# The modulation matrix's chunks leave the GLA stage for the two MLPs, and the first mixer takes its rest at a larger share

## The chip, the cores and the metric

The kernel runs on one core of a Trainium2 chip. The metric is the device time of one execution in microseconds (us); lower is better. Times of several executions are given as a median with the lowest and the highest.

## The reference, cut to what matters

Two transformer blocks of depth two run one after the other on 256 tokens of width 1024. The first block is attention, MLP, gated linear attention (GLA), MLP. The second block runs twice: a mixer (masked attention, a short convolution, gates) and a sparse expert stage. Before each of its two layers a conditioning vector `c` is turned into 6144 numbers, which shift, scale and gate that layer:

```python
# first block, depth 2
h = x
h = h + attention_mixer(rmsnorm(h, norm_mix[0]), ...)
h = h + sq_relu_mlp(rmsnorm(h, norm_mlp[0]), mlp_w_in[0], mlp_w_out[0])
h = h + gla_mixer(rmsnorm(h, norm_mix[1]), ...)
h = h + sq_relu_mlp(rmsnorm(h, norm_mlp[1]), mlp_w_in[1], mlp_w_out[1])
# second block, for l in range(2)
ada = (c @ w_ada[l] + b_ada[l])[:, None, :]
sh1, sc1, g1, sh2, sc2, g2 = jnp.split(ada, 6, axis=-1)
h = rmsnorm_2(x, norm1_g[l]) * (1.0 + sc1) + sh1
```

`w_ada` of both layers is 2 x 1024 x 6144 numbers of float32. It depends on nothing that the first block computes, so the kernel spreads `c @ w_ada` over the stages of the first block and the first mixer. The matrix is cut into 96 chunks of 128 rows x 1024 (512 KB each), 48 for each layer.

## The kernel before, in words

**Stages.** `run` goes through attention, MLP 0, GLA, MLP 1, mixer 0, expert stage 0, mixer 1, expert stage 1. Nearly all matmuls are products of a weight chunk with the activations. A weight chunk is 128 x 1024 float32 (512 KB), eight 128 x 128 tiles. `chunk` (L158 to L167) loads it on SP's queue into a buffer `raw`, lets ScalarE (ACT) round it to `whi` (L165) and VectorE (DVE) form the rest `wlo` (L166). `mm3` (L169 to L173) then takes three matmuls for each tile: `whi` with the high part of the activations (L171), `whi` with their low part (L172), `wlo` with the high part (L173). One chunk is 24 matmuls. There are 4 buffers `raw` and 3 each of `whi` and `wlo`; a load can only be issued when the chunk four loads before it has been used up.

**A modulation chunk** (`ada_steps`, L729 to L752) takes no matmul. Its load (L739) goes through the same 4 buffers `raw` and the same SP queue, and one DVE instruction multiplies it with `c` and sums along the row (L740) into one column of `mod`. L740 then frees the buffer.

**The background list.** The 96 modulation chunks are steps of the list `bg`, each at a cost of 1.14. Each time `lin` (L175) or `lin_nat` (L206) fetches a weight chunk it calls `bg.step(share)`, which adds `share` to a credit and issues steps from the list's head while the credit covers their cost. A share of 0.6 is about one modulation chunk for two weight chunks. `flush` issues whatever is left at once:

```python
def step(self, share):
    self.credit = self.credit + share if self.q else 0.0
    while self.q and self.credit >= self.q[0][0]:
        c, f = self.q.pop(0)
        self.credit -= c
        with self.net.tc.issue_after(self.net.last_lo):
            f()
```

`last_lo` is the `wlo` instruction of the weight chunk just fetched, so a modulation chunk is issued behind it. Within this the order of each engine's instructions is fixed when the program is built; at run time each engine goes through its own in order, and a waiting instruction holds those behind it.

**Who takes how many before.** MLP 0 (64 weight chunks, `MLP_SHARE` 0.6) takes 33 modulation chunks. The GLA stage replaces `bg` by a list of its own for its own DVE steps, and puts the first `GLA_ADA` = 8 modulation chunks behind them (L649); what that list has left when the last of the `wgin` chunks is fetched is flushed. The output projection of GLA (`wgo`, 8 weight chunks, L729) takes 4 more, MLP 1 takes 33, mixer 0 the last 18. Mixer 0 has 48 weight chunks ahead of its output projection `wout`; its list begins with 14 other steps of cost 0.45 (six empty ones, and eight that scale `x`, L775). With `MIX_SHARE` 0.45 its 47 calls give a credit of 21.2, of which 6.3 go to those steps and 14.9 to modulation chunks at 1.14 each: 13. The flush ahead of `wout` issues the other five. Mixer 1 runs the same code with an empty list.

**Names.** In the GLA stage, `v` and `r` come from `lin_nat` in PSUM and are taken out by L633, L634 (`vz`) and L643 to L645 (`sr`). The recurrence over the heads follows: L670 forms a state update, L677 (DVE) adds it to `st`; L684 forms scores, L685 (DVE) copies them under a mask to `at`. In mixer 0, L312 to L328 are the softmax, L829 the scores, L858 the copy of the transposed probabilities; L915 and L917 (DVE) form `ga`, L229 and L230 split it to `mh` and `ml`, which `wout` reads.

Of the kernel before, what the change touches and what calls it, by code (L numbers as in the profile page):

```python
# [20 lines left out]
T = 256  # L21
# [15 lines left out]
PACED = True  # L37
AHEAD = 100
WSLOTS = 4
MLP_SHARE = 0.6  # L40
MIX_SHARE = 0.45
U1_SHARE = 1.35
U2_SHARE = 1.45
V1_SHARE = 1.12
V2_SHARE = 0.52
DOTS = (8, 24)
SUMS = 4
GLA_ADA = 8
GSCALE = 2.0 ** 15
PACK = (("ones", 128), ("ident", 128), ("eps", 1), ("eps2", 1), ("one1", 1), ("gains64", 4), ("bada", 96))  # L50

# [49 lines left out]
class Net:  # L101
# [378 lines left out]
    def mlp(self, l):  # L480
        nc, a = self.nc, self.a
        with ExitStack() as st:
# [21 lines left out]
            self.early = factor  # L504
            self.lin(a["wmi"][l], 0, 32, 8, self.yh, self.yl, ev1, share=MLP_SHARE, n=T)
            if l == 0:
                self.next_norm(self.gain(1))
            else:
                while not self.ada0:
                    self.bg.q.pop(0)[1]()  # L510
                self.next_norm(self.gg, self.modc(0, 0), self.tot2, self.gain(4))
            self.lin(a["wmo"][l], 0, 8, 32, hh, hl, ev2, share=MLP_SHARE)


    def gla(self):
        nc, a, c, tc = self.nc, self.a, self.cst, self.tc
        with ExitStack() as st:
# [128 lines left out]
                                                   op0=ALU.add, op1=ALU.mult)  # L646
                return go

            self.bg.add(bg.q[:GLA_ADA])  # L649
            del bg.q[:GLA_ADA]  # L650
            for half in range(2):
                ci = self.lin_nat(a["wgin"], ci, 512, self.yh, self.yl, ev_v(half), 1.2)
            for half in range(2):
# [6 lines left out]
            oh, ol = [gp.tile([P, 8, T], F32R, tag=t, name=t) for t in ("oh", "ol")]  # L660
# [65 lines left out]
                pipe.push(h)  # L726
            pipe.drain()
            self.next_norm(self.gain(3))
            self.lin(a["wgo"], 0, 8, 8, oh, ol, self.add_x, n=T, share=MLP_SHARE)  # L729


    def ada_steps(self, l, i0, i1, cb):
# [48 lines left out]
    def mixer(self, l):  # L781
        nc, a, c, tc = self.nc, self.a, self.cst, self.tc
        with ExitStack() as st:
# [141 lines left out]
            ci = 0  # L925
            lin = lambda *args, **kw: self.lin(*args, share=MIX_SHARE, **kw)
            for nblk, ev in ((4, ev_k), (4, ev_v), (4, ev_q), (4, ev_c), (4, ev_h), (4, ev_b)):
# [558 lines left out]
```

## Time and profile before

| | before |
|---|---|
| device time, median of 3 (lowest to highest) | 2560.3 us (2559.42 to 2560.81) |
| the profiled execution's own time | 2562.75 us |
| its span in the profile | 2560.4 us |
| PE (matmul) busy | 2516.6 us, 98% |
| DVE busy | 2098.6 us, 82% |
| ACT busy | 1301.5 us, 51% |
| mean rate of all DMA | 221 GB/s |

The span runs from the first to the last instruction of the profiled execution; its own time has 2.35 us more around it. PE's busy time overlaps in itself, since matmuls are pipelined, so the places where it waits are read from its idle time, from the length of stages that do the same matmuls, and from the clock that it was granted, not from the busy share.

### The profile page before, as it was taken

How to read it: one execution, taken by the hardware profiler on the slowest of the kernel's cores; microseconds unless marked ns; L12 is line 12 of the kernel's file. 1: busy time of each engine (PE TensorE's matmuls, PEld its weight loads, DVE VectorE, ACT ScalarE, POOL GpSimd, SP SyncE). 2: the span in 40 equal slices, each digit the busy share in tenths (PEclk: the TensorE clock that was granted, in tenths of full speed). 3: DMA queues.
4: the chain of work that ended last, by engine and by line, in shares of the span. 5: the costliest groups of instructions: out<-in, count | busy, mean ns of one | idle time of the engine just before them, and what ended most of it. 6: DMA issues, size and time to landing. Idle time of an engine off the chain costs nothing.

```text
span 2560.4 us, 55126 instructions
## 1 busy us (share of the span) xinstructions
PE 2516.6 (98%) x22496; PEld 2461.7 (96%) x22496; DVE 2098.6 (82%) x3835; ACT 1301.5 (51%) x2031; POOL 182.3 (7%) x172
## 2 busy tenths in 40 slices
PE   8999999999998999999999999999999999999998
PEld 7799987999898999999999999999999999999998
DVE  7697687887787799889888777777798899888776
ACT  6654474554644645444444445645545444444444
POOL 0000100000000000321000121000000221000120
PEclk9999999999999999999999999999999999999999
DMA  5288754887477566877666887456566877666884
GB/s 191 86 293 281 253 183 153 268 275 264 149 251 234 159 195 200 295 259 247 212 185 203 265 296 242 140 178 197 165 191 204 299 249 265 194 190 199 280 296 164
DMA packets 155773, 566.47 MB, mean 221 GB/s; under 512 B 17680, under 2 KB 17904, under 8 KB 155264
## 3 DMA queue, kind: packets, MB, share of 16 engines
q1 hardware_dynamic: 135648, 490.97, 58.7%
q0 software_dynamic: 19872, 71.99, 9.0%
q8 instruction: 176, 2.88, 0.4%
q14 instruction: 77, 0.63, 0.1%
HBM read 561.83 MB, written 1.05 MB: 220 GB/s over the span
## 4 chain that ended last, share of the span: by engine, by line
PE 92%; DMA 3%; DVE 2%; ACT 1%; issue 1%; POOL 0%; SPq 0%; DVEq 0%; ACTq 0%
PE b L171 29%; PE b L173 29%; PE b L172 28%; PE b L1234 1%; PE b L1235 1%; DVE wlo L166 1%; DMA rows<-in_un,idx 1%; PE b L1181 1%; ACT whi L165 0%; DMA raw<-in_wmi 0%; PE b L829 0%; DMA raw<-in_wada 0%; DMA x<-in_xT 0%; PE b L426 0%; DMA A<-in_sel 0%
## 5 line engine op out<-in xcount | busy, mean ns | idle before, releaser
L171 PE MATMUL b<-yh,whi 128*128 128x224 f32 (+3 forms) x5336 | 1484.4, 279 | 12.1 <-ACT whi L165 11.4
L172 PE MATMUL b<-yl,whi 128*128 128x224 f32 (+3 forms) x5336 | 1476.2, 277 | 2.0 <-DVE yl L225 2.0
L173 PE MATMUL b<-yh,wlo 128*128 128x224 f32 (+3 forms) x5336 | 1476.2, 277 | 1.7 <-DVE wlo L166 1.5
L165 ACT CAST whi<-raw 128x1024 fp32r<-128x1024 f32 x829 | 868.4, 1049 | 1128.1 <-PE b L172 962.1
L166 DVE TENSOR_TENSOR wlo<-raw,whi 128x1024 fp32r<-128x1024 f32 x829 | 1009.9, 1220 | 260.0 <-ACT whi L165 254.6
L171 PEld LDWEIGHTS b<-yh,whi 128*128 128x128 f32 (+1 forms) x5336 | 1021.3, 192 | 17.5 <-ACT whi L165 12.7
L172 PEld LDWEIGHTS b<-yl,whi 128*128 128x128 f32 (+1 forms) x5336 | 1022.4, 192 | 4.9 <-DVE yl L225 2.4
L173 PEld LDWEIGHTS b<-yh,wlo 128*128 128x128 f32 (+1 forms) x5336 | 1021.0, 192 | 3.6 <-DVE wlo L166 2.7
L172 PE MATMUL b<-hl,whi 128*128 128x256 f32 x512 | 144.9, 283 | 0.0
L171 PE MATMUL b<-hh,whi 128*128 128x256 f32 x512 | 144.9, 283 | 0.0
L173 PE MATMUL b<-hh,wlo 128*128 128x256 f32 x512 | 144.9, 283 | 0.0
L1125 POOL DMA_INDIRECT rows<-in_un,idx x64 | 88.7, 1387 | 698.7 <-DVE gS L1093 411.1
L740 DVE CUSTOM_DVE_ANT_0 raw<-raw,c_cb 128x1024 f32<-128x1024 f32 x96 | 116.9, 1219 | 3.5 <-DMA raw<-in_wada 3.4
L1125 POOL DMA_INDIRECT rows<-in_ev,idx x64 | 69.4, 1084 | 613.7 <-DVE hN L1147 374.4
L172 PEld LDWEIGHTS b<-hl,whi 128*128 128x128 f32 x512 | 98.3, 192 | 0.0
L173 PEld LDWEIGHTS b<-hh,wlo 128*128 128x128 f32 x512 | 98.3, 192 | 0.0
L171 PEld LDWEIGHTS b<-hh,whi 128*128 128x128 f32 x512 | 98.3, 192 | 0.0
L1236 DVE TENSOR_TENSOR A<-A,b 128x512 f32<-128x512 f32 x112 | 73.5, 682 | 21.5 <-PE b L1235 21.3
L1206 ACT ACTIVATE A<-b 128x224 f32<-128x224 f32 x256 | 89.0, 348 | 0.0
L1136 DVE CUSTOM_DVE_ANT_0 rows<-rows,hN 128x1024 f32<-128x1024 f32 x64 | 78.0, 1219 | 12.4 <-DMA rows<-in_un,idx 12.4
L1147 DVE SCALAR_TENSOR_TENSOR hN<-rows,wS,hN 128x1024 f32<-128x1024 f32 x62 | 79.3, 1279 | 0.0
L1224 DVE TENSOR_TENSOR o<-oe,ghl 128x1024 f16<-128x1024 f16 x112 | 77.0, 688 | 1.7
(336 smaller groups left out, 2980.3 us busy)
## 6 DMA issues: line engine op xcount, KB each, us to landing
raw<-in_ut SPq DMA_DIRECT2D x256, 512.0 KB
raw<-in_ev SPq DMA_DIRECT2D x256, 512.0 KB
raw<-in_wada SPq DMA_DIRECT2D x96, 512.0 KB
raw<-in_win SPq DMA_DIRECT2D x80, 512.0 KB
raw<-in_wmi SPq DMA_DIRECT2D x64, 512.0 KB
raw<-in_wmo SPq DMA_DIRECT2D x64, 512.0 KB
raw<-in_wq SPq DMA_DIRECT2D x32, 512.0 KB
raw<-in_wgin SPq DMA_DIRECT2D x24, 512.0 KB
```

The costliest lines, as they stand in the source:

```text
L165: nc.scalar.copy(out=hi[:, :n], in_=raw[:, :n])
L166: self.last_lo = nc.vector.tensor_sub(out=lo[:, :n], in0=raw[:, :n], in1=hi[:, :n]).ins
L171: mm(out, lhsT=wh, rhs=yh, start=start, stop=False)
L172: mm(out, lhsT=wh, rhs=yl, start=False, stop=False)
L173: mm(out, lhsT=wl, rhs=yh, start=False, stop=stop)
L740: nc.vector.tensor_tensor_reduce(out=raw, in0=raw, in1=cb, op0=ALU.mult, op1=ALU.add, scale=1.0, scalar=0.0, accum_out=self.mod[:, i : i + 1])
L1125: nc.gpsimd.indirect_dma_start(out=got[g], out_offset=None, in_=a["un"] if name == "un" else a["ev"].rearrange("l i p d -> (l i p) d"), in ...
L1136: V.tensor_tensor_reduce(out=rows, in0=rows, in1=hN, op0=ALU.mult, op1=ALU.add, scale=1.0, scalar=0.0, accum_out=wS[:, g : g + 1])
L1147: V.scalar_tensor_tensor(out=hN, in0=rows, scalar=wS[:, g : g + 1], in1=hN, op0=ALU.mult, op1=ALU.add)
L1206: nc.scalar.activation(out=A[i2 // HALF][:, i2 % HALF, :], in_=ps[:, :NT], func=AF.Gelu_apprx_tanh)
L1224: V.tensor_tensor(out=o2, in0=e.unsqueeze(1).to_broadcast([P, 2, ng, HALF, GK]), in1=gates.to_broadcast([P, 2, ng, HALF, GK]), op=ALU.mult)
L1236: V.tensor_tensor(out=A[half][:, :, ts], in0=A[half][:, :, ts], in1=m.rearrange("p t i -> p i t"), op=ALU.mult)
```

## The change

The share of the MLPs goes from 0.6 to 0.72, that of the mixers from 0.45 to 0.55. The GLA stage puts no modulation chunk into its own list any more, and `wgo` takes none. By the credit and by the order of the loads, MLP 0 now takes 39 chunks, MLP 1 takes 40 and mixer 0 the last 17, against 33, 33 and 18 before, with 12 in the GLA stage. The changed credit of mixer 0 is 47 x 0.55 = 25.9; less the 6.3 it leaves 19.6, enough for 17 chunks at 1.14. What is computed does not change.

```diff
-MLP_SHARE = 0.6
-MIX_SHARE = 0.45
+MLP_SHARE = 0.72
+MIX_SHARE = 0.55
...
-GLA_ADA = 8
...
-            self.bg.add(bg.q[:GLA_ADA])
-            del bg.q[:GLA_ADA]
             for half in range(2):
                 ci = self.lin_nat(a["wgin"], ci, 512, self.yh, self.yl, ev_v(half), 1.2)
...
-            self.lin(a["wgo"], 0, 8, 8, oh, ol, self.add_x, n=T, share=MLP_SHARE)
+            self.lin(a["wgo"], 0, 8, 8, oh, ol, self.add_x, n=T)
```

The first place is DVE at the end of the GLA stage's `wgin` chunks. Before, it stands like this (L740 with `raw` is a modulation chunk, L166 the `wlo` of a weight chunk; the line `mod_69` behind each L740 with `raw` reads its sum out):

```order
L740 ISA raw_4396,mod_69<-raw_4396,c_cb_1315 128x1024
...
L740 ISA raw_4405,mod_69<-raw_4405,c_cb_1315 128x1024
L740 ISA mod_69 128x1
L677 SCALAR_TENSOR_TENSOR st_4432<-st_4425,eb_3878,b7_4427 128x256
L740 ISA raw_4408,mod_69<-raw_4408,c_cb_1315 128x1024
...
L677 SCALAR_TENSOR_TENSOR st_4436<-st_4429,eb_3877,b0_4434 128x256
L740 ISA raw_4411,mod_69<-raw_4411,c_cb_1315 128x1024
...
L645 SCALAR_TENSOR_TENSOR sr_3665<-rt_4386,rt2_4388 128x512
L685 COPY_PREDICATED at_3666<-c_gmask_3651,b1_4441 128x128
```

In the changed kernel the same place reads as follows; lines after the two removed constants and statements have moved up by one to three, so that L644 is L645 of before, L674 is L677, L682 is L685 and L165 is L166:

```order
L165 TENSOR_TENSOR wlo_4699<-raw_4696,whi_4698 128x1024
L165 TENSOR_TENSOR wlo_4734<-raw_4731,whi_4733 128x1024
L644 SCALAR_TENSOR_TENSOR sr_3683<-rt_4398,rt2_4400 128x512
L674 SCALAR_TENSOR_TENSOR st_4430<-st_4423,eb_3895,b0_4428 128x256
L682 COPY_PREDICATED at_3684<-c_gmask_3669,b1_4435 128x128
L644 SCALAR_TENSOR_TENSOR sr_3683<-rt_4403,rt2_4405 128x512
L682 COPY_PREDICATED at_3688<-c_gmask_3669,b5_4469 128x128
L165 TENSOR_TENSOR wlo_4770<-raw_4767,whi_4769 128x1024
```

The modulation chunks are gone from between the instructions that the recurrence needs, and the `wlo` of the first `wgo` chunks have moved up to their place.

The second place is DVE at the end of mixer 0, just ahead of `wout`, where the flush stands before (`wlo_9463` is the first `wout` chunk, L745 the sum with the bias when all 48 chunks of a layer are in):

```order
L740 ISA raw_9440,mod_69<-raw_9440,c_cb_1315 128x1024
L740 ISA mod_69 128x1
L298 COPY scc_9387<-b5_9355 128x2
L299 TENSOR_TENSOR sct_9386<-b5_9355,rstd_7404 128x256
L740 ISA raw_9443,mod_69<-raw_9443,c_cb_1315 128x1024
...
L915 SCALAR_TENSOR_TENSOR ga_7362<-ga_7362,b6_9391 128x256
L740 ISA raw_9446,mod_69<-raw_9446,c_cb_1315 128x1024
...
L915 SCALAR_TENSOR_TENSOR ga_7362<-ga_7362,b7_9417 128x256
L917 TENSOR_TENSOR ga_7362<-ga_7362,gc_7363 128x256
L166 TENSOR_TENSOR wlo_9463<-raw_9460,whi_9462 128x1024
```

In the changed kernel the last modulation chunk (`raw_9413`) stands here (L737 is L740 of before, L742 is L745):

```order
L165 TENSOR_TENSOR wlo_9410<-raw_9407,whi_9409 128x1024
L737 ISA raw_9413,mod_69<-raw_9413,c_cb_1315 128x1024
L737 ISA mod_69 128x1
L229 SCALAR_TENSOR_TENSOR ml_7364<-ga_7365,mh_7363 128x256 x2
L297 COPY scc_9366<-b4_9334 128x2
L298 TENSOR_TENSOR sct_9365<-b4_9334,rstd_7407 128x256
L742 TENSOR_TENSOR mod_69<-mod_69,c_pack_67 128x48
L290 TENSOR_SCALAR wyh_9456<-mod_69 128x8 x2
L165 TENSOR_TENSOR wlo_9463<-raw_9460,whi_9462 128x1024
```

No chunk is left for the flush: one modulation chunk, behind the last weight chunk of the projections ahead of `wout`, in place of a run of them.

The third place is SP's queue near the start of MLP 0. Before it loads one modulation chunk after two weight chunks:

```order
L162 DMA raw_1526<-in_wmi 128x1024
L162 DMA raw_1563<-in_wmi 128x1024
L739 DMA raw_1569<-in_wada 128x1024
L162 DMA raw_1603<-in_wmi 128x1024
L162 DMA raw_1640<-in_wmi 128x1024
L739 DMA raw_1646<-in_wada 128x1024
```

In the changed kernel (L161 and L736 are L162 and L739 of before) it is after one and two in turn for most of the way:

```order
L161 DMA raw_1526<-in_wmi 128x1024
L736 DMA raw_1532<-in_wada 128x1024
L161 DMA raw_1566<-in_wmi 128x1024
L161 DMA raw_1603<-in_wmi 128x1024
L736 DMA raw_1609<-in_wada 128x1024
L161 DMA raw_1643<-in_wmi 128x1024
L736 DMA raw_1649<-in_wada 128x1024
```

The loads have come closer: five modulation chunks for eight weight chunks.

## Rows read from the trace of the kernel before

**Rows 1.** The page, span and engines: busy us (share of the span) x instructions.

```profile
span 2560.4 us, 55126 instructions
PE 2516.6 (98%) x22496; PEld 2461.7 (96%) x22496; DVE 2098.6 (82%) x3835; ACT 1301.5 (51%) x2031; POOL 182.3 (7%) x172
```

**Rows 2.** Windows by stage; the first line names the columns.

```profile
core 0: us, PE busy (x) PEld busy (x) DVE busy (x) ACT busy (x) POOL busy (x), PEclk, DMA share, GB/s
...
114.50:206.90 92.40, 92.40 (x772) 92.34 (x771) 79.44 (x130) 52.43 (x96) 0.00 (x0) 1.00 0.81 273
206.90:299.20 92.30, 92.30 (x772) 92.28 (x771) 68.80 (x98) 39.35 (x51) 0.00 (x0) 1.00 0.83 276
438.60:535.80 97.20, 93.83 (x773) 92.50 (x772) 83.26 (x143) 54.10 (x101) 0.00 (x0) 1.00 0.81 269
...
627.90:791.20 163.30, 155.72 (x1238) 149.40 (x1236) 134.74 (x292) 85.20 (x151) 2.95 (x4) 0.98 0.64 208
1596.40:1749.30 152.90, 152.90 (x1236) 147.79 (x1235) 114.32 (x253) 85.28 (x154) 0.00 (x0) 1.00 0.51 159
791.20:816.80 25.60, 25.10 (x193) 24.81 (x194) 21.33 (x44) 16.25 (x27) 0.00 (x0) 0.91 0.66 211
1749.30:1772.40 23.10, 23.10 (x195) 23.10 (x194) 18.70 (x33) 15.43 (x26) 0.00 (x0) 1.00 0.57 183
```

**Rows 3.** PE's waits, end of mixer 0 (785 to 795): us, times, longest.

```profile
PE b L171 <- ACT whi L165: 5.9, 2, 5.4
```

**Rows 4.** L740 at the end of mixer 0 (776 to 800).

```profile
L740 DVE CUSTOM_DVE_ANT_0 raw<-raw,c_cb x6: 1212/1218/1226, 779.1 to 788.3; 128x1024 f32<-128x1024 f32 x6
```

**Rows 5.** L740 at the end of the GLA stage (360 to 395), its idle below.

```profile
L740 DVE CUSTOM_DVE_ANT_0 raw<-raw,c_cb x9: 1214/1218/1227, 371.3 to 390.0; 128x1024 f32<-128x1024 f32 x9
...
  DMA raw<-in_wada: 1.7, 3
```

**Rows 6.** Timeline of PE in the GLA recurrence, matmuls that waited.

```profile
383.45 1.13 PE L670 MATMUL b<-vz,kn 128*128 128x256 f32 x4 [0.41 <-DVE st L677]
...
385.93 1.11 PE L684 MATMUL b<-qe,ke 128*128 128x128 f32 x4 [1.34 <-DVE at L685]
...
391.70 0.70 PE L670 MATMUL b<-vz,kn 128*128 128x256 f32 x2 [1.43 <-DVE st L677]
```

**Rows 7.** Windows of 5 us there, columns as in rows 2.

```profile
375.00:380.00 5.00, 5.00 (x23) 4.11 (x22) 3.98 (x8) 0.37 (x1) 0.00 (x0) 1.00 0.98 363
...
385.00:390.00 5.00, 4.07 (x16) 3.45 (x16) 5.00 (x12) 3.07 (x5) 0.00 (x0) 0.66 0.80 249
```

**Rows 8.** PE's waits, start of MLP 1 (440 to 465).

```profile
PE b L171 <- ACT whi L165: 3.3, 4, 1.0
```

**Rows 9.** The chain, 360 to 470: start us, us, what; three landings.

```profile
383.03 4.58 DMA raw<-in_wada
...
434.43 6.49 DMA raw<-in_wmi
...
455.00 5.30 DMA raw<-in_wmi
```

**Rows 10.** ACT's waits in the first half of MLP 0 (100 to 197).

```profile
ACT whi L165 <- PE b L172: 21.6, 17, 5.0
ACT whi L165 <- DMA raw<-in_wmi: 8.7, 8, 2.4
```

**Rows 11.** The page's groups of instructions for L165 and L166.

```profile
L165 ACT CAST whi<-raw 128x1024 fp32r<-128x1024 f32 x829 | 868.4, 1049 | 1128.1 <-PE b L172 962.1
L166 DVE TENSOR_TENSOR wlo<-raw,whi 128x1024 fp32r<-128x1024 f32 x829 | 1009.9, 1220 | 260.0 <-ACT whi L165 254.6
```

**Rows 12.** PE's waits in mixer 0's attention (660 to 690).

```profile
PE b L829 <- ACT pT L858: 1.7, 1, 1.7
PE b L171 <- DVE smst L326: 0.6, 1, 0.6
```

## The prediction

> **What bounds the kernel now.** I read the page's head first. PE is busy for 98% of the span, DVE for 82% [rows 1], so moving DVE work can only pay where PE demonstrably waits or runs slowly. The busy share hides such places, so I then compared stages that do the same matmuls. Look in [rows 2] at the length and the matmul count of three pairs. The first halves of the MLPs have 772 and 773 recorded matmuls: 92.4 us in MLP 0, 97.2 in MLP 1. The mixers, from their first projection to the first `wout` matmul, have 1238 and 1236: 163.3 us with modulation chunks, 152.9 in mixer 1, which has none. `wout` takes 25.6 against 23.1. Where nothing disturbs, PE needs 92.3 us for 32 weight chunks, or 2.88 us for one; such stretches cannot become shorter. So the losses that this change can touch are 4.8 + 10.4 + 2.5 us in these pairs, and what lies in the GLA stage, which has no twin.
>
> **The change part by part.**
>
> **A, the end of mixer 0.** Before, L740 runs 6 times between 779.1 and 788.3 us [rows 4]. While these transfers hold the queue and the four `raw` buffers, the first `wout` chunk cannot be loaded. PE waits 5.9 us in two pieces for its rounding, 5.4 of it in one [rows 3]. The `wout` stage behind it had a mean granted clock of 0.91, and its twin 1.00 [rows 2]; so a part ran at the lower level of 1.2 GHz. The 5.4 us lie ahead of the stage and the other 0.5 inside it, so the whole loss is 5.4 + (25.6 - 23.1) = 7.9 us. In the changed order one modulation chunk stands there and the `wout` loads follow it at once; mixer 1 shows what is left then, a 23.1 us `wout` at full clock. I take 7.9. If the single wait goes but the lower clock stays, it is 5.4. The chunks taken out of the flush go earlier into the mixer, where they cost what E says.
>
> **B, the GLA recurrence.** DVE runs nine modulation chunks between 371.3 and 390.0 us at 1.22 us each, 11.0 us in all, and stands 1.7 us more for their data [rows 5]. It goes in order, so L677 and L685 queue behind them, and PE waits for exactly these two: 0.41 + 1.34 + 1.43 = 3.18 us [rows 6]. From 385 to 390 us the granted clock was 0.66, so 5 x 0.34 = 1.7 us of full clock were missing, while PE waited for 1.34 us of it [rows 7]. All of both would be 4.9 us. If the L645 and L166 instructions that now stand there still cause the longest wait, and the clock stays low, the gain is 3.18 - 1.43 = 1.8 us. I take 4.0, nearer to the upper end, because nine of DVE's instructions go and the three waits name DVE. `wgo` loses its modulation chunks too; they lie beside its matmuls, and its remaining small waits come from three output blocks finishing together, so I count nothing for it.
>
> **C, the start of MLP 1.** Behind `wgo`, whose loads share the ring with modulation chunks, MLP 1 starts with too little weight at hand. PE waits 3.3 us in four pieces for `whi` [rows 8], and the half is 4.8 us longer than its twin [rows 2], which follows a projection without modulation chunks. After the change MLP 1 follows such a projection as well. I take 4.8, with the price of the denser mix in D. Zero is the lower end, if the start is short for another reason.
>
> **D, the MLPs.** What is moved must fit here: 33 to 39 and 33 to 40 L740, so 6 and 7 more at 1.22 us, 7.3 and 8.5 us of DVE work. In the first half of MLP 0, DVE is busy 79.4 of 92.4 us [rows 2]; three to four more chunks make it 84, still below. The tighter thing is the ring of four `raw` buffers. MLP 1 now passes 64 + 40 = 104 chunks in 92.4 + 92.3 = 184.7 us, so that a buffer may be held 4 x 184.7 / 104 = 7.10 us on average. A weight chunk holds it for its landing, then 1.05 us of ACT and 1.22 of DVE [rows 11]; a modulation chunk for its landing and 1.22. Landings on the chain are 4.58 and 5.30 us, and once 6.49 [rows 9]. With 4.58 the mean is (64 x 6.85 + 40 x 5.80) / 104 = 6.45 us, well inside. With 5.30 it is 7.17, 1% too long: 1.7 us for an MLP. So the steady part costs from 0 to 1.7 us each; in between, 0.
>
> Bandwidth does not forbid it: the MLPs need 104 x 0.524 MB in 184.7 us, 295 GB/s, and the queue carried 363 in a 5 us stretch of modulation chunks alone [rows 7]. The start is thin, though. Eight casts in the first half of MLP 0 waited for data, 2.4 us at most [rows 10], and PE felt none of it: three `whi` chunks are in hand, and two chunks of matmuls, 5.8 us, cover the 2.3 us of rounding and 2.4 of lateness with 1.1 to spare. The changed order puts one more modulation transfer ahead of the sixth or seventh weight chunk. At its share of the budget, 7.10 / 4 = 1.8 us, that is 0.7 us more than is to spare. I take 0.6 for each MLP, 1.2 together, with 0 and 3.4 as bounds.
>
> One rule speaks against this. The landing that began at 383 us, close behind the 5 us in which the queue carried 363 GB/s [rows 7], took 4.58 us, the shortest of the three [rows 9]. The Trainium skill (DMA: Bandwidth & Descriptors, Latency and other measured facts) says that the HBM access latency is 0.2 us on average and 2 us at high load, and that it makes most of a transfer's fixed cost. By that rule, as an estimate, denser loading could add up to 1.8 us to a landing of 4.58, for a mean hold of 8.25 us, some 30 us for each MLP and a time near 2604. The trace disagrees at the place where the load was highest, and the sum goes by the trace.
>
> **E, mixer 0's attention.** PE waits 1.7 + 0.6 us there [rows 12], for a softmax whose DVE steps share the engine with the scaling of `x` and with modulation chunks. In the new order two modulation chunks stand in that stretch in place of one, and two scaling steps have left it. From all of the 2.3 us going to two L740 on the path, 2 x 1.22 = 2.4 us more, I take 0: what comes and what goes there are about as long.
>
> **The sum.** -7.9 - 4.0 - 4.8 + 1.2 + 0 = -15.5 us. The profiled execution has its span of 2560.4 us and an own time of 2562.75, so it would come to 2547.3. It stands 2.45 us above the median of 2560.3, so the median goes to **2544.8 us**.
>
> **The rivals.**
>
> **The ring becomes the bound (slower).** If landings grow with the denser mix, PE follows the four `raw` buffers through both MLPs. With 6.49 us, the longest on the chain [rows 9], the mean hold is 8.36 us, 18% above 7.10: 33 us for each MLP, and 2560.3 + 65 - 16.7 = 2609. The gain is used up when the MLPs lose 8.35 us each, 4.5%; a hold of 7.42 us, or landings of 5.55 on average, decides it. For it: the landings of 5.30 and 6.49 come from the first part of MLP 1 and the stretch ahead of it, that is from this kind of load. Against: both stand where one stage gives way to the next, and the steady part of MLP 0 ran at full speed with a budget of 4 x 184.7 / 97 = 7.62 us, which landings of 5.30 fill to 7.21.
>
> **The GLA waits have another cause.** L677 and L685 also read what PE has just made, and `sr` has to be taken out on DVE at the same place. Then B is near 0 and the time is 2548.8. Against: DVE's queue is full of L740 at that very time.
>
> **The stall of mixer 0 moves into its middle.** DVE is busy 134.7 of 163.3 us there [rows 2], and the projections now carry 17 chunks where 13 went before the flush. If the attention loses 2.4 us and as much again at a lower clock, and C is only half, the gain is 15.5 - 4.8 - 2.4 = 8.3 us: 2552.
>
> **The change doesn't do what it says.** A flush could remain ahead of `wout`. The order excludes it: all 96 chunks are loaded ahead of the first `wout` load.
>
> **How the numbers follow.** A measurement of this kernel can tell about 0.2%, or 5.1 us, from no change. Forecast and its near kin (2540 to 2550, the second rival in it): 0.60. The third rival, or a smaller sum of the same kind (2550 to 2555): 0.20. A ring that eats most of it (within 5.1 us of before): 0.12. The ring as the bound, slower by more: 0.08. So faster 0.80, same 0.12, slower 0.08. All upper values together, with the attention's 2.3 us, are 7.9 + 4.9 + 4.8 + 2.3 = 19.9: 2540.4; all lower ones leave 5.4 + 1.8 + 0 - 3.4 - 2.4 = 1.4: 2558.9. The range is **2540 to 2556**, which leaves out the ring rival and the last of the losses, and nearly nothing below.
>
> **What the changed profile would show.** A: no wait of some us ahead of `wout`, and its stage at 23 us with clock 1.00. B: no L740 between 300 and 430 us, and PE's waits on L677 and L685 below 1 us. C: MLP 1's first half near 92.4 us. D: more casts waiting for data in the MLPs (before, 8 in the first half of MLP 0), PE waits on L165 there of about 1 us; the halves longer than 93 us would show the ring. E: waits in mixer 0's attention near 2.3 us. The prediction is wrong if the MLP halves grow by several us, or if the waits of GLA stay with DVE free of L740.

## The result and the profile after

| | before | after |
|---|---|---|
| device time, median of the session | 2559.86 us | 2541.97 us (six executions, 2539.25 to 2545.3) |
| the profiled execution's own time | 2562.75 us | 2544.02 us |
| its span | 2560.4 us | 2542.3 us |

The ratio is 0.9935, with a 95% interval of 0.9925 to 0.9944. The change takes off 17.9 us; 2544.8 us was predicted, in a range of 2540 to 2556. One execution of before took 4196.81 us and is not in the ratio; without it before's median is 2559.42 us and the gain 17.5.

In the changed kernel the line numbers are lower by one up to the two lines that left the GLA stage: the rounding is L164 and L165, the three matmuls L170 to L172. Behind them they are lower by three, so that the modulation sum is L737, and in the recurrence the state update is L667 with `st` at L674, the scores L681 with `at` at L682. Where an experiment adds lines there, these shift: `st` is L676 in e3, L679 in e10, L681 in e11.

The page's head, to set against [rows 1]:

```profile
span 2542.3 us, 55095 instructions
PE 2509.7 (99%) x22496; PEld 2457.8 (97%) x22496; DVE 2096.9 (82%) x3835; ACT 1301.9 (51%) x2031; POOL 182.6 (7%) x172
```

Each engine works off as many instructions as before, and DVE is busy as long (2098.6 us before). The span has lost 18.1 us and PE's busy time 6.9, so 11.2 us were gaps on PE. The 6.9 are about what the clock gives: over the whole span the mean granted clock rose from 0.995 to 0.998, some 7 to 8 us of 2550. Not all of that is the change's, as B below shows. Windows of the changed kernel by stage, with the same columns as [rows 2]: in order of time the two halves of MLP 0, the GLA stage with `wgo`, the two halves of MLP 1, mixer 0 and its `wout`; then two pieces of 5 us inside the GLA stage.

```profile
114.60:208.60 94.00, 92.91 (x772) 92.44 (x771) 82.33 (x134) 50.90 (x93) 0.00 (x0) 1.00 0.83 279
208.60:300.90 92.30, 92.30 (x771) 92.29 (x771) 73.15 (x107) 40.38 (x54) 0.00 (x0) 1.00 0.88 297
300.90:433.40 132.50, 130.74 (x798) 110.17 (x796) 94.04 (x148) 81.57 (x128) 6.95 (x14) 1.00 0.45 139
433.40:528.90 95.50, 92.98 (x772) 92.31 (x771) 84.25 (x146) 53.09 (x96) 0.00 (x0) 1.00 0.82 282
528.90:621.40 92.50, 92.40 (x770) 92.19 (x769) 74.82 (x111) 42.27 (x57) 0.00 (x0) 1.00 0.87 292
621.40:775.50 154.10, 153.48 (x1238) 148.22 (x1237) 134.93 (x302) 86.11 (x152) 2.96 (x4) 1.00 0.70 229
775.50:798.60 23.10, 23.10 (x195) 23.10 (x194) 18.72 (x35) 15.43 (x26) 0.00 (x0) 1.00 0.61 188
...
380.00:385.00 5.00, 4.95 (x27) 4.07 (x26) 4.27 (x10) 3.70 (x8) 0.00 (x0) 1.00 0.31 105
385.00:390.00 5.00, 5.00 (x31) 3.80 (x32) 3.30 (x14) 0.85 (x3) 0.00 (x0) 1.00 0.33 105
```

Set each stage against the same stage of before, cut at the same matmuls of PE (the end of attention's projection, the first and the last matmul on `hh`, the last of `wgo`, the first and the last of `wout`, the end of the query projection behind it):

| stage | before | after | difference |
|---|---|---|---|
| MLP 0, halves | 92.4, 92.1 | 94.0, 92.1 | +1.6 |
| GLA and `wgo` | 139.6 | 132.6 | -7.0 |
| MLP 1, halves | 97.1, 92.1 | 95.5, 92.5 | -1.3 |
| mixer 0 up to `wout` | 163.3 | 154.1 | -9.2 |
| `wout` | 25.5 | 23.0 | -2.5 |
| the query projection | 55.6 | 56.7 | +1.1 |

These differences and 0.1 us ahead of MLP 0 make 17.1 of the 18.1 us that the span lost; the remaining 1.0 lies behind, where both kernels run the same program. The query projection has the same program too; in this execution a stretch of it, from 813.5 us, ran at the lower clock of 1.2 GHz, and before had none there.

PE's waits of the changed kernel in the first half of MLP 0, the first half of MLP 1 and mixer 0's attention (engine, line, what for, us in total, times, longest):

```profile
PE b L170 <- ACT whi L164: 1.1, 1, 1.1
...
PE b L170 <- ACT whi L164: 2.5, 3, 1.4
...
PE b L170 <- DVE sm L835: 0.3, 1, 0.3
```

In the first half of MLP 0 before had no wait (PE is busy for all of its 92.40 us in [rows 2]); the second row answers to [rows 8] (3.3 us), the third to the 2.3 us of [rows 12]. Between 770 and 800 us, the place of [rows 3], the view lists no wait. ACT's waits for data in the changed kernel, first in the window of [rows 10], then from end to end of that half:

```profile
ACT whi L164 <- DMA raw<-in_wmi: 28.3, 20, 3.0
...
ACT whi L164 <- DMA raw<-in_wmi: 30.3, 22, 3.0
```

Where 8 casts waited for their data, for 8.7 us in all, 20 do now, for 28.3 us. PE felt 1.1 us of it.

### The profile page after: what moved, and what is told of

Read it like the earlier page. It is cut to its first block, busy times and chain, and to the rows that moved or that the text cites. A ratio compares the mean times of both kernels' runs of the same rounds, so it can differ in the third digit from the quotient of the medians.

```text
span 2542.3 us, 55095 instructions
## 1 busy us (share of the span) xinstructions
PE 2509.7 (99%) x22496; PEld 2457.8 (97%) x22496; DVE 2096.9 (82%) x3835; ACT 1301.9 (51%) x2031; POOL 182.6 (7%) x172
## 4 chain that ended last, share of the span: by engine, by line
PE 89%; DMA 4%; DVE 3%; ACT 2%; issue 1%; POOL 0%; SPq 0%; DVEq 0%; ACTq 0%
PE b L170 28%; PE b L172 28%; PE b L171 27%; DMA raw<-in_wmo 2%; DVE wlo L165 1%; PE b L1231 1%; ACT whi L164 1%; PE b L1232 1%; DMA raw<-in_wmi 1%; DMA rows<-in_un,idx 1%; PE b L1178 1%; PE b L826 0%; DVE raw L737 0%; PE b L425 0%; DMA raw<-in_wada 0%
## 5 line engine op out<-in xcount | busy, mean ns | idle before, releaser
L170 PE MATMUL b<-yh,whi 128*128 128x224 f32 (+3 forms) x5336 | 1481.1, 278 | 12.2 <-ACT whi L164 11.7
L172 PE MATMUL b<-yh,wlo 128*128 128x224 f32 (+3 forms) x5336 | 1474.9, 277 | 1.3 <-DVE wlo L165 1.2
L164 ACT CAST whi<-raw 128x1024 fp32r<-128x1024 f32 x829 | 868.6, 1050 | 1113.0 <-PE b L171 854.5
L165 DVE TENSOR_TENSOR wlo<-raw,whi 128x1024 fp32r<-128x1024 f32 x829 | 1010.3, 1220 | 258.0 <-ACT whi L164 253.5
L170 PEld LDWEIGHTS b<-yh,whi 128*128 128x128 f32 (+1 forms) x5336 | 1020.0, 191 | 16.4 <-ACT whi L164 12.6
L172 PEld LDWEIGHTS b<-yh,wlo 128*128 128x128 f32 (+1 forms) x5336 | 1019.5, 191 | 4.0 <-DVE wlo L165 2.4
L172 PE MATMUL b<-hh,wlo 128*128 128x256 f32 x512 | 145.0, 283 | 0.1
L170 PE MATMUL b<-hh,whi 128*128 128x256 f32 x512 | 144.9, 283 | 0.0
L737 DVE CUSTOM_DVE_ANT_0 raw<-raw,c_cb 128x1024 f32<-128x1024 f32 x96 | 117.1, 1220 | 2.8 <-DMA raw<-in_wada 2.7
L1122 POOL DMA_INDIRECT rows<-in_ev,idx x64 | 69.6, 1088 | 613.5 <-DVE hN L1144 374.2
L172 PEld LDWEIGHTS b<-hh,wlo 128*128 128x128 f32 x512 | 98.3, 192 | 0.3 <-DVE wlo L165 0.3
L170 PEld LDWEIGHTS b<-hh,whi 128*128 128x128 f32 x512 | 98.3, 192 | 0.0
L1233 DVE TENSOR_TENSOR A<-A,b 128x512 f32<-128x512 f32 x112 | 73.3, 683 | 20.1 <-PE b L1232 19.9
L1133 DVE CUSTOM_DVE_ANT_0 rows<-rows,hN 128x1024 f32<-128x1024 f32 x64 | 78.1, 1220 | 11.3 <-DMA rows<-in_un,idx 11.2
```

Of the source, the lines that this page charges most:

```text
L164: nc.scalar.copy(out=hi[:, :n], in_=raw[:, :n])
L165: self.last_lo = nc.vector.tensor_sub(out=lo[:, :n], in0=raw[:, :n], in1=hi[:, :n]).ins
L170: mm(out, lhsT=wh, rhs=yh, start=start, stop=False)
L172: mm(out, lhsT=wl, rhs=yh, start=False, stop=stop)
L737: nc.vector.tensor_tensor_reduce(out=raw, in0=raw, in1=cb, op0=ALU.mult, op1=ALU.add, scale=1.0, scalar=0.0, accum_out=self.mod[:, i : i + 1])
L1122: nc.gpsimd.indirect_dma_start(out=got[g], out_offset=None, in_=a["un"] if name == "un" else a["ev"].rearrange("l i p d -> (l i p) d"), in ...
```

## The experiments

The theory under test had the prediction's five terms A to E. Times are medians; each ratio is to executions of before on the same chip.

**e1: the kernel before with the mixer's share alone.**

```diff
-MIX_SHARE = 0.45
+MIX_SHARE = 0.55
```

> The kernel before with only the mixers' share raised to 0.55: GLA, wgo and MLPs keep their chunks, mixer 0 its 18, of which 2 in place of 6 stand in a row ahead of wout. Theory (the run of chunks ahead of wout makes PE wait and lowers its clock, and the earlier order of chunks and scaling steps also relieves the attention): from the first mixer projection to the end of wout 178 to 181 us in place of 188.9, and the whole 8 to 11 us below the kernel before, about 2550. Rival (the mixer gained because the stages ahead of it changed): the mixer stays within 2 us of 188.9 and the whole within 3 us of before.

Measured: 2546.21 us, ratio 0.9946 (0.9929 to 0.9962). Its windows for a piece of the GLA stage, mixer 0 and `wout`:

```profile
320.00:325.00 5.00, 5.00 (x27) 4.67 (x28) 1.65 (x2) 3.34 (x4) 0.00 (x0) 0.66 0.01 5
625.70:779.10 153.40, 153.11 (x1238) 147.97 (x1237) 134.26 (x294) 86.28 (x152) 2.95 (x4) 1.00 0.70 226
779.10:803.80 24.70, 23.79 (x194) 23.20 (x193) 19.86 (x43) 15.71 (x26) 0.00 (x0) 1.00 0.62 192
```

Mixer and `wout` take 178.1 us, against 188.8 before and 177.1 after. One number, 0.55, brings 12.6 us, a little more than the 8 to 11 expected; 10.7 of them are in the mixer and `wout`, and the rest lies in stages whose program is that of before. e2, below, holds the other parts of the change and gains 7.5, so the two together come to 20.1 where the whole change has 17.9; the difference is within the intervals of the ratios.

**e2: the changed kernel with the mixer's share put back.**

```diff
-MIX_SHARE = 0.55
+MIX_SHARE = 0.45
```

> The changed kernel with the mixers' share back at 0.45: 17 chunks in mixer 0, 5 of them in a row ahead of wout. Theory: the wait ahead of wout, the low clock and the attention's wait all come back; first projection to end of wout 186 to 189 us in place of 177.2, the whole 9 to 12 us above the changed kernel, about 2552; GLA and MLPs as in the changed kernel to 0.5 us. Rival (mixer 0 gained because chunks left it, or by what runs ahead of it): below 181 us and the whole within 4 us of the changed kernel.

Measured: 2551.29 us, ratio 0.9971 (0.996 to 0.9982). PE's waits from mixer 0's attention to `wout`:

```profile
PE b L170 <- ACT whi L164: 3.6, 2, 3.0
PE b L826 <- ACT pT L855: 1.7, 1, 1.7
PE b L170 <- DVE smst L325: 0.6, 1, 0.6
```

Mixer and `wout` are back at 187.6 us. The flush ahead of `wout` costs a wait again, and the attention has the same two waits as [rows 12], to a tenth. Two stretches at the lower clock, at 673.5 and 782.7 us, came back as well; before has them at 679.6 and 788.9.

**e8: the attention's order alone.** In the changed kernel the list's 14 early steps get a cost of 0.55, so that at a share of 0.55 they go out call for call as they did at 0.45.

```diff
-        self.bg.q[:0] = [(0.45, lambda: None)] * 6 + [(0.45, lambda b=b: scale(b)) for b in range(ND)]
+        self.bg.q[:0] = [(0.55, lambda: None)] * 6 + [(0.55, lambda b=b: scale(b)) for b in range(ND)]
```

> The changed kernel with the 14 steps ahead of mixer 0's modulation chunks at a cost of 0.55 in place of 0.45, so that the scaling steps and the first modulation chunk stand in the attention where they stood before the change; 2 chunks stand in a row ahead of wout. Theory (the attention's wait of 2.3 us and the low clock behind it come from scaling steps and a modulation chunk standing between the softmax steps of the last heads): both come back, mixer 0 up to wout is 157 to 159 us in place of 154.1, the whole 3 to 5 us above the changed kernel. Rival (the attention was relieved by its timing against the weights, not by the order of those steps): mixer 0 stays below 155.5.

Measured: 2546.12 us, ratio 0.9959 (0.9945 to 0.9973). PE's waits in mixer 0's attention:

```profile
PE b L826 <- ACT pT L855: 1.7, 1, 1.7
PE b L170 <- DVE smst L325: 0.6, 1, 0.6
```

The mixer takes 156.6 us in place of 154.1, and `wout` 24.8 in place of 23.0 (two modulation chunks now stand in a row ahead of it). So where the list's steps stand in the attention is worth about 2.5 us. The 156.6 lie between the 157 to 159 of the theory and the rival's 155.5: both waits came back, the lower clock, which the theory had return with them, did not.

**e3: the eight modulation chunks back in the GLA stage.**

```diff
+            self.bg.add(bg.q[:8])
+            del bg.q[:8]
             for half in range(2):
```

> The changed kernel with 8 modulation chunks back in the GLA stage's list (mixer 0 then has 9 instead of 17), none in wgo. Theory (L740 holds up DVE's recurrence steps): from the last matmul of MLP 0 to the last of wgo 138 to 140 us in place of 132.6; PE waits on L677 and L685 of 2 to 4 us return, so does a low clock near 386 us; MLP 1 as in the changed kernel. The whole 5 to 7 us above the changed kernel, if mixer 0 with fewer chunks gains less than 1. Rival (it was the modulation chunks beside wgo, or other DVE work, that cost GLA its time): 132.6 stays within 1 us.

Measured: 2550.41 us, ratio 0.9962 (0.9948 to 0.9976). GLA with `wgo` takes 138.7 us in place of 132.6, with no stretch at the lower clock (one there near 386 us was expected). The whole stands 8.4 us above the changed kernel, more than the 5 to 7 expected; part of that lies where the chunks do not reach, such as MLP 1's second half, 94.0 us in this trace in place of 92.5. Two windows of this kernel, to set against the same two of the changed kernel above, then PE's waits, then a piece of DVE's timeline (start us, us, engine, line, operation; in brackets the idle time before it):

```profile
380.00:385.00 5.00, 2.48 (x10) 1.58 (x11) 4.38 (x12) 1.25 (x2) 0.00 (x0) 1.00 0.97 345
385.00:390.00 5.00, 3.85 (x18) 2.40 (x17) 5.00 (x9) 2.77 (x5) 0.00 (x0) 1.00 0.74 250
```

```profile
PE b L669 <- DVE st L676: 2.2, 4, 0.8
PE b L683 <- DVE at L684: 1.3, 1, 1.3
PE b L698 <- DVE A L687: 0.6, 1, 0.6
```

```profile
378.80 1.23 DVE L739 CUSTOM_DVE_ANT_0 raw<-raw,c_cb 128x1024 f32<-128x1024 f32 x1 [0.18 <-DMA raw<-in_wada]
...
379.95 0.48 DVE L676 SCALAR_TENSOR_TENSOR st<-st,eb,b 128x256 f32<-128x256 f32 x1
380.63 1.23 DVE L739 CUSTOM_DVE_ANT_0 raw<-raw,c_cb 128x1024 f32<-128x1024 f32 x1 [0.21 <-DMA raw<-in_wada]
...
381.78 0.48 DVE L676 SCALAR_TENSOR_TENSOR st<-st,eb,b 128x256 f32<-128x256 f32 x1
382.68 1.23 DVE L739 CUSTOM_DVE_ANT_0 raw<-raw,c_cb 128x1024 f32<-128x1024 f32 x1 [0.41 <-DMA raw<-in_wada]
...
...
384.43 0.49 DVE L684 COPY_PREDICATED at<-c_gmask,b 128x128 f32<-128x128 uint32 x2
```

Here 28 matmuls run in ten microseconds where the changed kernel has 58. The first two `st` stand behind a modulation sum each, and that sum has waited for its own transfer. B is real, and it is worth 6.1 us at full clock: 4.2 us are in the three listed waits and the `oh` and `whi` waits of `wgo` are unchanged; the other 1.9 us stand in no wait that the trace lists.

**e10 and e11: which half of a modulation chunk costs it.** e10 puts eight loads at the places of the chunks, each followed by a DVE operation on one column; e11 puts eight multiply-and-sum operations there, which write to a `raw` buffer and have no load.

```diff
...
+                nc.sync.dma_start(out=raw, in_=a["wada"][i])
+                nc.vector.tensor_scalar_mul(raw[:, :1], raw[:, :1], 1.0)
...
```

```diff
...
+                nc.vector.tensor_tensor_reduce(out=raw, in0=self.cst["cb"], in1=self.cst["cb"], op0=ALU.mult,
+                                               op1=ALU.add, scale=1.0, scalar=0.0, accum_out=dum)
...
```

> The changed kernel with eight more loads of 512 KB in the GLA stage's list, at the places where the kernel before has its modulation chunks, each followed by a DVE operation on one column alone, so that only the loads and the buffers they hold come back, not the 1.2 us of multiply-and-sum. If the chunks cost the GLA stage their time on DVE's queue (my theory for B): the stage with the projection stays at 132.5 to 134 us. Rival (the loads take buffers and bandwidth from the projection's own loads): 137 to 139 us, as with all of the chunk back (138.7).

> The changed kernel with eight more multiply-and-sum operations on DVE, 128x1024 each, in the GLA stage's list, at the places of the kernel before's modulation chunks, on a tile that is in place already: DVE's time comes back without a load. My theory for B: the stage with the projection takes 136.5 to 139 us (138.7 with all of the chunk back), and TensorE waits again for the recurrence's state. Rival (the loads and buffers): it stays at 132.5 to 134 us. Between the two, 134.5 to 136.5 us, both have a part.

Measured: e10 2540.79 us, ratio 0.9934 (0.9917 to 0.9951); e11 2543.71 us, ratio 0.9938 (0.9922 to 0.9953). GLA with `wgo` takes 133.7 us with the loads alone and 135.6 with the sums alone, and 1.5 of the latter lie ahead of the first sum, where a stretch ran at the lower clock (320 to 330 us have a granted clock of 0.83 there, 1.00 in the changed kernel). PE's waits between 375 and 395 us, e10 first:

```profile
PE b L701 <- DVE A L690: 0.2, 1, 0.2
PE b L672 <- DVE st L679: 0.2, 1, 0.2
```

```profile
PE b L674 <- DVE st L681: 1.0, 1, 1.0
```

Neither theory held alone. The loads add 1.1 us, the sums 3.0 (1.5 without that stretch), both together 6.1. DVE's waits for these loads between 365 and 395 us, e3 first, then e10:

```profile
DVE raw L739 <- DMA raw<-in_wada: 1.7, 4, 0.9
```

```profile
DVE raw L651 <- DMA raw<-in_wada: 6.4, 5, 1.5
```

So the surplus is not DVE's wait for the transfers as such: in e10 DVE stands 6.4 us for them, with its queue behind it, and the stage loses 1.1; in e3 it stands 1.7, and the stage loses 6.1. Nor is it the length of the sums as such: in e11 the eight run between 372.9 and 388.3 us and never wait, and other work fills in between. It takes the load and the sum in one step. The order of DVE's other instructions differs between these kernels as well: e3 has an `st` behind each of two late sums, e10 has its five waits ahead of the first `st`. How much of the surplus is that order stays open.

**e4: `wgo` gets its modulation chunks back.**

```diff
-            self.lin(a["wgo"], 0, 8, 8, oh, ol, self.add_x, n=T)
+            self.lin(a["wgo"], 0, 8, 8, oh, ol, self.add_x, n=T, share=MLP_SHARE)
```

> The changed kernel with modulation chunks back beside wgo only (5 of them; mixer 0 then has 12). Theory (MLP 1 starts short of weights because the loads behind wgo share the ring with modulation chunks): the first half of MLP 1 goes from 95.5 us to 97 or more, and from the last matmul of MLP 0 to the last of wgo stays at 132.6 to 133.5. The whole 1 to 3 us above the changed kernel. Rival (what is left at the start of MLP 1 has nothing to do with wgo: it is its own dense mix of loads): the half stays within 0.6 us of 95.5 and the whole within 1 us.

Measured: 2550.2 us, ratio 0.9958 (0.9941 to 0.9975); the five executions fall into two groups, 2542.73 and 2543.97 us and three between 2550.2 and 2550.91, and the profile is of the lower one. I did not find what parts them. GLA with `wgo` takes 132.9 us and MLP 1's first half 95.8, against 132.6 and 95.5. The rival held for the half; the theory wanted 97 or more.

**e5: a later start in the MLPs.** The first eight weight chunks of each first half carry no modulation chunk, and the share is 0.82, which leaves each MLP 40.

```diff
-                    if self.early is None:
+                    if self.early is None and b >= skip:
...
-MLP_SHARE = 0.72
+MLP_SHARE = 0.82
```

> The changed kernel with no modulation chunk beside the first 8 weight chunks of each MLP and the MLPs' share at 0.82 behind them: 40, 40 and 16 chunks. Theory (what the MLPs lose is at their starts, where a thin stock of weights meets the denser loads): the first halves go from 94.0 and 95.5 us to 92.4 to 93, the second halves stay below 93, and the whole is 3 to 4.5 us below the changed kernel, about 2538. Rival (the steady ring of four buffers is at its limit already): at the higher share the second halves or the ends of the first grow, the four halves together stay above 373 us (374.2 in the changed kernel), and the whole is not below it by 2 us.

Measured: 2549.65 us, ratio 0.997 (0.9959 to 0.9981). The four halves:

```profile
114.00:206.40 92.40, 92.40 (x773) 92.34 (x772) 78.67 (x128) 50.88 (x94) 0.00 (x0) 1.00 0.81 270
206.40:304.00 97.60, 94.28 (x771) 92.72 (x770) 76.53 (x114) 40.33 (x53) 0.00 (x0) 1.00 0.89 293
438.00:530.70 92.70, 92.61 (x773) 92.35 (x771) 79.00 (x136) 50.98 (x94) 0.00 (x0) 1.00 0.81 267
530.70:627.30 96.60, 94.08 (x771) 92.64 (x770) 79.20 (x119) 43.65 (x59) 0.00 (x0) 1.00 0.88 301
```

The starts are cured, and the second halves now lose 5.4 and 4.1 us, as the rival had it. They move 293 and 301 GB/s, about the changed kernel's 297 and 292: with more to move at much the same rate they take longer.

**e7: more in the MLPs.** A share of 0.88 empties the list before mixer 0 (48 chunks in each MLP).

```diff
-MLP_SHARE = 0.72
+MLP_SHARE = 0.88
```

> The changed kernel with the MLPs' share at 0.88: 48 chunks in each MLP, none in mixer 0. Theory (a buffer may now be held 4 x 184.7 / 112 = 6.6 us, which landings of 4.7 us already fill): the MLPs become bound by the ring, each 4 to 12 us longer than 184.7, mixer 0 1 to 2 us shorter than in the changed kernel; the whole 6 to 20 us above the changed kernel, 2548 to 2562. Rival (the ring has room, since landings stay at 4.6 us at any load): the MLPs lose below 2 us each and the whole is within 3 us of the changed kernel.

Measured: 2570.65 us, ratio 1.0048 (1.003 to 1.0065), slower than before. The second halves:

```profile
210.40:314.10 103.70, 98.46 (x791) 95.63 (x792) 80.51 (x124) 40.44 (x53) 0.00 (x0) 1.00 0.87 291
...
548.40:650.70 102.30, 96.06 (x772) 93.23 (x771) 81.09 (x123) 43.30 (x58) 0.00 (x0) 1.00 0.87 293
```

The four halves take 403.9 us where the changed kernel takes 374.2, at the same 291 to 293 GB/s, and DVE is free for a fifth of the time. The MLPs lose 17 and 18 us, more than the 4 to 12 expected for each.

**e6: five `raw` buffers.** To make room, four work tiles of the GLA and expert stages get one buffer each in place of two, so only its MLPs are read, not its whole time (2551.02 us).

```diff
-        raw = self.sp.tile([P, 1024], F32, tag="raw", name="raw", bufs=4)
+        raw = self.sp.tile([P, 1024], F32, tag="raw", name="raw", bufs=5)
...
```

> The changed kernel with five raw buffers in place of four; to make room for the fifth, GLA's two evacuation tiles and the expert stages' two one-hot tiles have one buffer in place of two, so only the MLPs are read, not the whole. Theory (the number of buffers holds the loads back, not the DMA queue): casts that wait for data in the MLPs fall from 20 to 30 in a half to below 10, PE's waits on them (1.1 and 2.5 us) to below 0.5, and the first halves to 92.4 to 93 us. Rival (the DMA queue itself is the limit at 290 to 300 GB/s): as many casts wait, and the halves stay at 94 to 95.5.

The first half of MLP 0, the second, and the same of MLP 1; then ACT's wait for data in the first of them, to set against the 22 casts above:

```profile
114.20:206.60 92.40, 92.40 (x772) 92.35 (x772) 83.22 (x138) 52.13 (x96) 0.00 (x0) 1.00 0.86 289
206.60:298.70 92.10, 92.10 (x770) 92.10 (x769) 71.27 (x102) 39.16 (x50) 0.00 (x0) 1.00 0.86 294
430.40:523.60 93.20, 92.59 (x773) 92.33 (x772) 84.31 (x147) 52.49 (x96) 0.00 (x0) 1.00 0.85 291
523.60:615.70 92.10, 92.10 (x770) 92.10 (x769) 74.77 (x110) 42.69 (x57) 0.00 (x0) 1.00 0.87 299
```

```profile
ACT whi L164 <- DMA raw<-in_wmi: 6.5, 4, 2.5
```

With the same chunks all four halves come to within 1.1 us of 92.1, and 4 casts wait for data where 22 did. What makes weights late in the changed MLPs is that four buffers are too few for the time that each is held, not the queue's rate, which is about the same here.

**e9 and e12: is there a better split?** e9 leaves the first four weight chunks of each first half free (as in e5, with `skip=4`) and raises the mixer's share to 0.68; e12 has shares of 0.66 and 0.80.

```diff
-MIX_SHARE = 0.55
+MIX_SHARE = 0.68
...
```

```diff
-MLP_SHARE = 0.72
-MIX_SHARE = 0.55
+MLP_SHARE = 0.66
+MIX_SHARE = 0.8
```

> The changed kernel, but the first four chunks of each MLP's first half carry no modulation chunk, and the first mixer's share is 0.68: 37, 38 and 21 chunks by the order of loads. My theory (the MLPs' loss under the change is at the start of a half, where the buffers have had no slack yet, and the mixer still has slack): the two first halves fall from 94.0 and 95.5 us to 92.3 to 93, the second halves stay at 92.1 to 92.7, the mixer up to the output projection stays at 153 to 156 us and the projection at 23.0, and the whole comes to 2537 to 2541 us. Rival (the mixer's start is as tight as an MLP at that share): the mixer takes 157 to 160 us and the whole stays at 2542 to 2546 us.

> The changed kernel with an MLP share of 0.66 and a mixer share of 0.80: 36, 36 and 24 chunks by the order of loads. If a smaller share all along is as good as a later start: the four MLP halves come to 92 to 94 us each (sum 370 to 372, against 374.2 in the changed kernel), the mixer to 154 to 157 us, the whole to 2538 to 2543 us. Rival (the start of a half costs the same 1.5 to 3 us at any share, and the mixer at 0.80 has a chunk beside nearly every load and is slowed): first halves 94 to 95.5 us, mixer 157 to 161 us, the whole 2544 to 2549 us.

Measured: e9 2544.55 us, ratio 0.9942 (0.9929 to 0.9954); e12 2547.25 us, ratio 0.9954 (0.994 to 0.9968). The first halves of the two MLPs and mixer 0 in e12, then its modulation sums in the attention, between 640 and 690 us (count, ns of one, first and last start):

```profile
113.50:206.30 92.80, 92.77 (x773) 92.37 (x772) 81.01 (x133) 52.48 (x96) 0.00 (x0) 1.00 0.83 276
431.00:524.00 93.00, 92.57 (x772) 92.31 (x771) 81.97 (x142) 52.79 (x96) 0.00 (x0) 1.00 0.81 278
...
616.20:781.50 165.30, 158.73 (x1237) 150.10 (x1237) 142.78 (x315) 86.29 (x152) 2.96 (x4) 0.99 0.71 231
```

```profile
L737 DVE CUSTOM_DVE_ANT_0 raw<-raw,c_cb x7: 1212/1218/1219, 641.0 to 679.7; 128x1024 f32<-128x1024 f32 x7
```

The MLPs got what I expected (e12: 92.8, 92.1, 93.0, 92.2 us; e9: 92.4, 92.1, 93.1, but 95.4 in the last half). The mixer gave more back: 165.3 us in e12 and 158.5 in e9, against 154.1. In e12 seven sums stand in the attention from 641.0 to 679.7 us; the changed kernel has three there, from 658.5 to 682.7. e9's rival was right. In e12 the theory was right on the MLPs and the rival on the whole; the mixer went beyond the 157 to 161 us of the rival (the mean clock of 0.99 there tells of a stretch at the lower one). Neither beats the changed kernel, and no version that I ran does by a measurable amount.

## Why the prediction came out right, and where it was off

The total was right to 2.8 us, and the mechanism of A and the place of B were right. Of the single terms only A has its size; the others made up for each other, so that the total came so close is in part luck.

**A, the end of mixer 0: right.** -7.9 was predicted. The 5.4 us wait is gone and `wout` takes 23.0 us, 2.5 less. e2 brings it back with the flush.

**B, the GLA recurrence: too small.** -4.0 was taken, with 4.9 as the upper bound; the stage lost 7.0, and e3 shows 6.1 for the eight chunks alone. The same windows in before and then in the changed kernel, cut at PE's matmuls: from the start of the stage to the first matmul of `v` and `r`, and from the last of these to the end of `wgo`.

```profile
299.06:331.93 32.87, 32.87 (x238) 30.49 (x236) 16.37 (x22) 19.30 (x24) 6.95 (x14) 0.95 0.58 170
380.70:438.63 57.93, 53.20 (x345) 43.16 (x344) 44.02 (x100) 26.81 (x60) 0.00 (x0) 0.97 0.45 147
```

```profile
300.79:332.18 31.39, 31.39 (x238) 29.01 (x236) 16.38 (x22) 19.27 (x24) 6.95 (x14) 1.00 0.59 185
380.08:433.37 53.29, 51.69 (x349) 42.59 (x348) 36.78 (x88) 26.86 (x63) 0.00 (x0) 1.00 0.26 79
```

The recurrence with `wgo` lost 4.6 us, inside the bound, and `v` and `r` 0.9. The other 1.5 lie ahead of them, where neither kernel has a modulation chunk on DVE and before ran a stretch at the lower clock, from 321.2 us. The bound had no place for these two pieces. The 1.5 are not firmly the change's: e1 has such a stretch there with the old GLA stage, e5, e7 and e11 have one with the new, and e3 has none with the chunks. That adding up listed waits is too little shows in e3 too, where they hold 4.2 of 6.1 us at full clock. Nothing was counted for `wgo`, and e4 bears that out with 0.3.

**C, the start of MLP 1: too large.** I read -4.8 from one execution. e1 runs the same program up to there, and its half took 95.5 us where before took 97.1. Six traces with the changed kernel's MLPs and `wgo` (after, e2, e3, e8, e10, e11) give 93.8 to 95.5, and 94.6 in the mean. With the start left clear or the mix thinner it is 92.7, 93.1 and 93.0 (e5, e9, e12). So the chunks that left this place were worth about 96.3 - 92.9 = 3.4 us, and the denser mix took about 94.6 - 92.9 = 1.7 back. e4 makes the cause that I named less clean: with five chunks beside `wgo` again the half took 95.8, only 1.2 more than that mean. My reading, argued and not shown, is that both sources shorten the same stock of weights, so that taking one away doesn't restore it while the other is there.

**D, the MLPs: right in kind, too small.** 0.6 us was taken for each start, and the starts cost about 1.7 each. In seven traces with the changed kernel's program up to there (those six and e4), MLP 0's first half took 93.5 to 94.6 us, 94.1 in the mean, against 92.4 in before and in e1, so that is no chance of one execution. The steady part cost nothing in MLP 0's second half and 0.4 us in MLP 1's, within its bounds of 0 and 1.7; in other traces of the same program it cost up to 0.7 (e2) and 1.8 (e3). By the prediction's own sign, halves over 93 us, the ring does show, at the two starts. The budget of 7.10 us for holding a buffer proved to be the edge, not a line well ahead: the changed kernel's second half of MLP 0 moves 297 GB/s, which is 52 loads in 92.3 us and four buffers held 7.1 us. e5 and e7 put more in and get no more GB/s (55 and 57 loads in their second halves of 97.6 and 103.7 us, 7.1 and 7.3 us for a buffer), and with five buffers (e6) the lateness goes. The step that failed here is the sum for the hold: it had landing, ACT and DVE back to back. In that half of MLP 0 weights landed in 4.8 us and modulation chunks in 4.5, in the median; by the prediction's sum that holds a buffer for 6.6 us, an estimate, so some 0.5 us of each turn lies elsewhere (the traces do not say where), and the room that the sum left was not there. The rival "the ring becomes the bound" was wrong for 0.72 and is what happens by 0.82.

The trace decides on the rule that I weighed there as well. Landings of the weight loads in the second half of MLP 0, at 297 GB/s:

```profile
DMA to landing us min/median/max: 3.5/4.8/6.4
```

The Trainium skill (DMA: Bandwidth & Descriptors, Latency and other measured facts) gives a higher HBM latency at high load, which as an estimate meant landings of up to 6.4 us and 30 us more for each MLP. Single landings reach that size, but the median is 4.8 here and 4.7 for the `wmo` loads in the same half of e1, at 276 GB/s: at these rates the trace does not bear the rule out.

**E, the attention of mixer 0: taken as nothing, and it was a gain.** I took 0 between -2.3 and +2.4, "what comes and what goes there are about as long". The mixer lost 9.2 us, 5.4 of them A's, so E is -3.8. The waits of 2.3 us shrank to 0.3, and e8 brings back both, 1.7 and 0.6, with the order of the early steps alone: that is worth 2.5 us. What the count of instructions in a stretch doesn't show is where in it they stand. The rest, about 1.3 us, goes with the lower clock at 679.6 us that the changed kernel lacks; e2 has it again and e8 not, so its cause stays open. What failed is the step from how many steps stand in the stretch to what they cost.

Measured, by the prediction's own terms: A -7.9, B -7.0, C with D -1.3 + 1.6, E -3.8, and +1.1 - 1.0 + 0.1 of the stages that were not touched, -18.2 in all (the span's -18.1, with rounding) against -15.5. Of these 18.2 the 1.5 us of B at 321 us and the 1.3 of E at 679.6 are lower clock that no run shows to be the change's.

## What to carry to other kernels

A list of fill-in work has a right amount for each stage, and the stage's first chunks show the limit before the busy shares or the bandwidth do; divide buffers x the stage's time by its loads, and compare that with the time a load holds a buffer. Price a fill-in step whole and in its place: here eight loads alone cost a recurrence 1.1 us, eight sums alone 1.5, and the two together 6.1. And read a twin of the same stage in several executions before its difference becomes a term of a sum: 1.6 us of one of these terms was the spread of the same program.

## What had not been expected of the hardware

Short stretches at the lower clock came and went where the program was the same: the query projection behind `wout` took 53.6 us without one (e1, e3, e10) and 56.7 with one (after, e11), 3.1 us that no change in these kernels aims at (it is not the only thing that moves there: before took 55.6 without one). Whoever compares single traces should set such a stretch apart first. And the mean rate of all DMA stayed within 302 GB/s in every MLP half, with 36 modulation chunks in an MLP or with 48.
